# The fallback for crowded experts moved behind the last expert, one-hot matrices right behind the slots, and half of the router's logits amid the output projection

## The chip, the cores and the metric

The kernel runs on one core of a Trainium2 chip. The metric is the device time of one execution in microseconds (us); the time of a kernel is the median of several executions. The profile and the trace come from one further execution that the hardware profiler recorded. Engines are named PE (TensorE, with PEld for its weight loads), DVE (VectorE), ACT (ScalarE), POOL (GpSimd) and SP (SyncE, which here only issues DMAs).

## The reference

256 tokens of 1024 channels go through two layers of four parallel mixers, gates and an output projection, each followed by a feed-forward part (dense in layer 0, a mixture of experts in layer 1), and then through a second block. What the change touches is the end of layer 1's mixers and the experts:

```python
def first_block(x, ...):
    for l in range(2):
        h = _rmsnorm(x, norm_mix[l])
        ...                                   # four mixers, gates: merged
        x = x + merged @ w_out[l]
        h = _rmsnorm(x, norm_ffn[l])
        if l == 0: x = x + _swiglu(h, ffn_w1, ffn_w3, ffn_w2)
        else:      x = x + _moe_ffn(h, router, moe_w1, moe_w3, moe_w2)
    return x

def _moe_ffn(h, router, w1, w3, w2):          # 256 tokens, 8 experts of width 1408
    logits = h @ router
    top_logit, top_idx = lax.top_k(logits, 2)
    gates = softmax(top_logit)
    # each token: sum over its two experts e of gate * (silu(h@w1[e]) * (h@w3[e])) @ w2[e]

def second_block(x, ...):
    h = rms_norm(x, norm_gain)
    proj = h @ w_in                           # "w_in_2" below
    ...
```

Every product is formed to float32's accuracy.

## The kernel before

**Products.** A weight block is loaded by a DMA that SP issues (`raw`), rounded by ACT into a high part `wh` and split by DVE into the rest `wl`. An activation has a high and a low part as well (`mh`, `ml`; `hr` in two halves; `xg`). Each block product is then three PE instructions: high by high, low by high, high by low. All of PE's instructions pass through the helper `mm` or `TE.transpose` (line 123 in the profile); a trace row is told apart by its tiles, the result left of the arrow and the operands right of it. PSUM has banks under two tags, "mm" and "mx", four each. Names in rows of `dense` products: `mh,wh` is w_out, `wh,xg` an expert's first and third matrix, `wh,mu` its second, `nr,wh` and `wh,nr` the second block's w_in_2.

**The end of layer 1's mixers.** `dense` forms `merged @ w_out` in two groups of 512 channels (g = 0, 1); `residual` (L980) adds each to `xT`, which holds the tokens' stream as 8 channel tiles of 128x256. Group 0 gives the tiles 0 to 3, group 1 the tiles 4 to 7.

**The router.** For each channel tile ACT scales it (`hT`, L1393), DVE squares it (`msq`, L1395), two narrow products with the router's table `rt` and with a column constant add to the logits and to the sums of squares, and two transposes put the tile into token rows. All eight tiles go through this behind w_out's last product. ACT copies the sums (`part`), PE folds them (`c_moe,part`), and DVE chooses two experts for each token in a chain of 128x16 operations (L1423 to L1432, ending in the mask `msk`) while POOL forms the norm's factor `mrs` with a power. PE counts with `msk` each token's place in its expert, DVE writes it as `pos`; `cnt` and `cnti` are the largest expert's number of tokens. `hr` is the normalised rows, two halves of width and two of tokens.

**The fallback.** An expert's tokens are gathered into at most 128 places. A path for any number (the body of `tc.If(full > P)`, L1573) is compiled in and stands between the counts and the gates: every engine loads the count `cnti` into a register (L1570) and branches. With these inputs no expert has over 128 tokens and every engine jumps over the body.

**The experts.** `gather` builds for two experts a one-hot matrix `Q` (DVE, L1478) from `pos`, multiplies it with `hr` (PE, `Q,hr`), and casts the result into `xg` (ACT and DVE). `ffn` runs one expert and gives `y` (ACT L1552 and DVE L1553), scaled by the gates `gs`; `scatter` multiplies `y` with the transposed one-hot matrix `pt_` and adds to `xT` (DVE L1568). While expert 7 runs its last blocks, w_in_2's first blocks are loaded already. The second block's norm then squares `xT` (`room`), sums it over the partitions (`ones,room`), takes POOL's power and transposes the factors (`c_id,nrmb`); w_in_2's products with the tiles `nr`, which need no factor, are put around this.

The order on each engine is set by a list scheduler with priorities; `tc.high_priority(offset=...)` lifts instructions, `add_manual_dep` forbids an order, and each engine then works through its row in order.

Of the kernel before, what the change touches and what calls it, by code (L numbers as in the profile page):

```python
# [21 lines left out]
# TensorE takes its instructions in order: (step of the chains, products of the gates put before it)  # L22
# [7 lines left out]
# where each constant lies: name -> (group, first column, columns)  # L30
# [3 lines left out]
def _constants():  # L34
# [12 lines left out]
    for m in (2, 4, 8, 16, 32):  # L47
# [20 lines left out]
           "mfold": np.arange(P)[:, None] % 32 == np.arange(16)[None, :], "col8": np.broadcast_to(np.arange(32) == 8, (P, 32))}  # L68
# [6 lines left out]
    for g, blocks in (("c_id", ident), ("c_mix", mix), ("c_moe", moe), ("c_nsa", nsa)):  # L75
# [25 lines left out]
def build(tc, I, out, dbg=None, upto=99):  # L101
# [15 lines left out]
    # TensorE, with a list of its instructions where one is asked for  # L117
# [18 lines left out]

    last_in = {}
# [69 lines left out]
    def wsplit(raw, k, n, perm=False):  # L207
        """hi / lo tiles [128, k, n] of a loaded [128, k, n] block."""
# [20 lines left out]
        # own slots, the standing ones after the first of them, own slots  # L229
# [41 lines left out]
    def wload_(src, k, n, rows, pinned):  # L271
        """src: DRAM [k*128, n] -> raw tile [128, k, n]."""
# [17 lines left out]
    def wstream(W, c0, cn, K, perm=False, rows=False, raw=None, pre=None):  # L290
        """hi, lo, kc-base, count for the rows of W[:, c0:c0+cn]."""
# [16 lines left out]
    def dense(W, c0, cn, K, act, jobs, perm=False, rows=False, raw=None, pre=None):  # L308
        """jobs: ("T", off, n): out[n cols, 256 tok]; ("R", off, n): out[tok, n] of both token tiles.
        Returns per job an AP: T -> [n, 256], R -> list of two [128, n]."""  # L310
# [3 lines left out]
        for kind, off, n in jobs:  # L314
            if kind == "T":
                if used + T > 512:
                    cur, used = bank("mm"), 0
# [4 lines left out]
            else:  # L322
                aps = []
                for j in range(2 if kind == "R" else 1):
                    if used + n > 512 or n == 512:
                        cur, used = bank("mm"), 0
# [26 lines left out]
    def inv_sqrt(pool, sums, n, mul, add, nm):  # L353
        """PSUM sums [128, n] -> (sums * mul + add) ^ -0.5, or of the larger of both when mul is None."""
# [25 lines left out]
    def head_scale(pool, sq, n, mul, add, nm):  # L380
        """sq [128 = 2 heads x 64, n tokens] -> PSUM [128, n]: the same per head and token."""
# [59 lines left out]
    def ln_rows(mp, y, eps_v, nm):  # L441
        """y: [128, 8, 64] in place: (y - mean) * rstd over the last axis."""
# [32 lines left out]
    def mix_layer(l):  # L475
        with ExitStack() as ls_:
# [4 lines left out]
            branch = {}  # L481
            tmp = lambda shape, nm, tag: mp.tile(shape, F32, name=nm, tag=tag)
# [4 lines left out]
            # ---- projections of the RWKV branch, shifted and mixed  # L487
# [30 lines left out]
            # ---- RWKV: decays and keys, channels on partitions  # L518
# [18 lines left out]
            S.activation(out=ls, in_=ls, func=AF.Exp)            # decay up to the step before  # L537
# [6 lines left out]
            ar = mp.tile([P, 2, 2, 2, P], F32, name="ar")        # [ch, b, token tile, a|r, tok]  # L544
# [18 lines left out]
            # ---- rows of the same  # L563
            br, kr, vr = t2("br", "pt0"), t2("kr", "pt1"), t2("vr", "pt2")       # [tok, tile, channel]
# [13 lines left out]
            def solve(j):  # L578
                """Scores of token tile j and the solve (I - A)^-1 of its two chunks."""
# [15 lines left out]
                # right-hand sides [A~ | Aak V]  # L595
# [30 lines left out]
                # state side, the part without the running state  # L626
                nt = mp.tile([P, 2, 2, 64], F32, name="nt", tag="nt", bufs=2)   # [k', chunk, b, k]
# [21 lines left out]
                # query side  # L649
# [37 lines left out]
            def rows_to_branch(y, i, th, tl):  # L687
                """y [128 tok, (tile, head), 64] -> branch i, transposed, hi/lo."""
# [39 lines left out]
            # ---- projections of the other branches  # L728
# [1050 lines left out]
```

## Time and profile before

| | |
|---|---|
| median of 3 executions | 1457.94 us (1456.82 to 1458.63) |
| profiled execution, span | 1455.6 us |
| PE busy | 1410.7 us, 97% |
| DVE busy | 1092.4 us, 75% |
| ACT busy | 822.3 us, 56% |
| POOL busy | 63.9 us, 4% |
| DMA moved | 294.46 MB, 202 GB/s |

The span is the time from the first to the last instruction of the profiled execution, which is 2.3 us under the median of the three timed ones. A duration in the trace is of that execution. PE rows overlap: a product's row shows 0.28 or 0.39 us, and the next one starts 0.12 or 0.23 us after it, so for PE the starts are read.

### The profile page before, as it was taken

How to read it: one execution, taken by the hardware profiler on the slowest of the kernel's cores; microseconds unless marked ns; L12 is line 12 of the kernel's file. 1: busy time of each engine (PE TensorE's matmuls, PEld its weight loads, DVE VectorE, ACT ScalarE, POOL GpSimd, SP SyncE). 2: the span in 40 equal slices, each digit the busy share in tenths (PEclk: the TensorE clock that was granted, in tenths of full speed). 3: DMA queues.
4: the chain of work that ended last, by engine and by line, in shares of the span. 5: the costliest groups of instructions: out<-in, count | busy, mean ns of one | idle time of the engine just before them, and what ended most of it. 6: DMA issues, size and time to landing. Idle time of an engine off the chain costs nothing. (4 is left out here: it accounts for less than half of the span.)

```text
span 1455.6 us, 25080 instructions
## 1 busy us (share of the span) xinstructions
PE 1410.7 (97%) x10183; PEld 1304.4 (90%) x10183; DVE 1092.4 (75%) x1606; ACT 822.3 (56%) x1169; POOL 63.9 (4%) x82
## 2 busy tenths in 40 slices
PE   5999999999999999999999799999999999999998
PEld 5999999999999899999899688888888887998997
DVE  3759876776655575797676799898898998676665
ACT  4644264564444464433645588788788777465553
POOL 1000010001000100001000000000000001120000
PEclk9999999999999999999999899999999999999999
DMA  7453024576553445421458599899799895843342
GB/s 255 151 176 116 31 92 168 177 290 206 199 186 127 152 132 170 145 84 34 143 182 289 180 359 361 299 358 361 282 371 358 288 340 171 280 142 117 116 117 87
DMA packets 137388, 294.46 MB, mean 202 GB/s; under 512 B 6718, under 2 KB 28614, under 8 KB 137009
## 3 DMA queue, kind: packets, MB, share of 16 engines
q1 hardware_dynamic: 133952, 282.64, 56.3%
q0 software_dynamic: 3232, 10.13, 2.1%
q8 instruction: 81, 1.33, 0.4%
q14 instruction: 43, 0.34, 0.1%
q10 hardware_dynamic: 80, 0.02, 0.0%
HBM read 290.15 MB, written 2.62 MB: 201 GB/s over the span
## 5 line engine op out<-in xcount | busy, mean ns | idle before, releaser
L253 DVE TENSOR_TENSOR wl<-raw,wh 128x1024 fp32r<-128x1024 f32 (+1 forms) x542 | 633.5, 1186 | 221.7 <-ACT wh L252 216.7
L252 ACT CAST wh<-raw 128x1024 fp32r<-128x1024 f32 (+1 forms) x542 | 549.0, 1021 | 384.9 <-PE mm L123 293.2
L123 PE MATMUL mm<-hh,wh 128*128 128x256 f32 x1376 | 395.8, 288 | 4.1 <-ACT hh L1650 3.8
L123 PE MATMUL mm<-hl,wh 128*128 128x256 f32 x1376 | 393.4, 286 | 0.2 <-DVE hl L205 0.2
L123 PE MATMUL mm<-hh,wl 128*128 128x256 f32 x1376 | 392.7, 286 | 0.0
L123 PEld LDWEIGHTS mm<-hh,wh 128*128 128x128 f32 x1376 | 264.3, 192 | 9.7 <-ACT hh L1650 4.0
L123 PEld LDWEIGHTS mm<-hl,wh 128*128 128x128 f32 x1376 | 264.1, 192 | 3.1 <-issue 1.8
L123 PEld LDWEIGHTS mm<-hh,wl 128*128 128x128 f32 x1376 | 264.1, 192 | 2.0 <-issue 1.2
L123 PE MATMUL mm<-wh,xg 128*128 128x512 f32 (+1 forms) x768 | 231.5, 376 | 0.0
L123 PEld LDWEIGHTS mm<-wh,xg 128*128 128x128 f32 x768 | 142.7, 188 | 21.9
L123 PE MATMUL mm<-wl,xg 128*128 128x512 f32 (+1 forms) x384 | 143.9, 375 | 0.0
L123 PE MATMUL mx<-wh,mu 128*128 128x512 f32 x352 | 118.4, 398 | 0.0
L123 PEld LDWEIGHTS mm<-wl,xg 128*128 128x128 f32 x384 | 72.2, 188 | 11.2
L123 PEld LDWEIGHTS mx<-wh,mu 128*128 128x128 f32 x352 | 66.2, 188 | 13.5
L123 PE MATMUL mx<-wl,mu 128*128 128x512 f32 x176 | 69.3, 394 | 0.0
L886 DVE SCALAR_TENSOR_TENSOR cac<-cu,pcd,cac 128x256 f32<-128x256 f32 x120 | 52.2, 476 | 0.0
L123 PE MATMUL mx<-uh,wh 128*128 128x256 f32 x176 | 48.8, 280 | 0.4 <-ACT uh L204 0.4
L123 PE MATMUL mx<-ul,wh 128*128 128x256 f32 x176 | 49.1, 280 | 0.0
L123 PE MATMUL mx<-uh,wl 128*128 128x256 f32 x176 | 49.1, 279 | 0.0
L123 PE MATMUL mm<-nr,wh 128*128 128x256 f32 x192 | 39.3, 302 | 3.4 <-ACT nr L410 1.7
L123 PEld LDWEIGHTS mx<-wl,mu 128*128 128x128 f32 x176 | 33.1, 188 | 5.9
L123 PE MATMUL mm<-mh,wl 128*128 128x256 f32 x128 | 35.9, 281 | 0.0
(681 smaller groups left out, 2183.7 us busy)
## 6 DMA issues: line engine op xcount, KB each, us to landing
raw<-in_moe_w_dram SPq DMA_DIRECT2D x104, 1024.0 KB
raw<-in_w_in_dram SPq DMA_DIRECT2D x44, 1024.0 KB
raw<-in_ffn_w_dram SPq DMA_DIRECT2D x33, 1024.0 KB
raw<-in_w_gate_dram SPq DMA_DIRECT2D x32, 1024.0 KB
raw<-in_moe_w_dram SPq DMA_DIRECT2D x32, 768.0 KB
raw<-in_w_out_dram SPq DMA_DIRECT2D x12, 1024.0 KB
raw<-in_w_branch_dram SPq DMA_DIRECT2D x8, 1024.0 KB
raw<-in_moe_w_dram SPq DMA_DIRECT2D x8, 512.0 KB
```

Source lines behind the costliest of these rows:

```text
L123: i = getattr(nc.tensor, name)(*a, **k)
L252: a = S.copy(out=h, in_=raw)
L253: i = V.tensor_sub(out=o, in0=raw, in1=h)
L886: V.scalar_tensor_tensor(acc[:, b], cu[:, b, 2 + k:2 + k + T], dw[:, 2 * k + b:2 * k + b + 1], acc[:, b], op0=OP.mult, op1=OP.add)
```

## The change

Four things change.

1. The fallback becomes a function `beyond`, called by expert 7's `ffn` between its last product with w2 and its `y`. `y`'s two banks then have the tag "mm", and inside the body `dense` uses "mx". The count's register is loaded under a high priority as expert 7 begins.
2. The first `gather` is started before the gates, at a high priority: `Q` directly behind `pos`. Three of the four low parts of `hr` are forced behind it. The four small operations that give the count move into `gates`.
3. The router's work on the tiles 0 to 3 (`routed(.., 0, ..)`: 4 scalings, 2 squares, 8 narrow products, 8 transposes) is recorded into w_out's group 1 of layer 1, and a manual dependence puts it ahead of that group's last products. The tiles 4 to 7 stay behind.
4. The column constant gets a table of its own (`c_col`). It and the router's table are loaded twice, by POOL's queue, once for each half.

```diff
             for g in range(2):
+                rec[0] = filler = []
                 _, bb = dense(I["w_out"][l], g * 512, 512, KC, (mh, ml), TJ)
+                if g and l == 1:
+                    rec[0] = chain = []
+                    late["routed"] = r_ = {"lg": bank("mm"), "rows": [[bank()] for _ in range(2)]}
+                    half = [mg.tile([P, 512], F32, name="gth", tag="gth", bufs=13) for _ in range(4)]
+                    routed(r_, 0, [x.rearrange("p (a b) -> p a b", b=T) for x in half])
+                    for i in chain:
+                        tc.add_manual_dep(filler[60].ins, i.ins.name, nosync, reason="first half first")
+                rec[0] = None
...
+    def router(pool):
+        late["rt"] = rt = pool.tile([P, KC, 32], F32, name="rt")
+        G.memset(rt, 0.0)
+        nc.gpsimd.dma_start(out=rt[:, :, 0:8], in_=I["router"][0].rearrange("(k p) e -> p k e", p=P))
+        cload("c_col", pool, nc.gpsimd)
+
+    def routed(r_, hf, tiles):
+        lg, rows, rt = r_["lg"], r_["rows"], late["rt"]
+        gain = gains("nf", 1, 2)
+        hT, sq = tiles[:2], tiles[2:]
+        for q in range(2):
+            for c in range(2):
+                k = 4 * hf + 2 * q + c
+                S.activation(out=hT[q][:, c], in_=xT[:, k], func=AF.Copy, scale=gain[:, k:k + 1])
+            V.tensor_tensor(out=sq[q], in0=xT[:, 4 * hf + 2 * q:4 * hf + 2 * q + 2], in1=xT[:, 4 * hf + 2 * q:4 * hf + 2 * q + 2], op=OP.mult)
...
+            lg, rows = late["routed"]["lg"], late["routed"]["rows"]
+            for x in rows:
+                x.append(bank())
+            routed(late["routed"], 1, [hT[:, 2 * q:2 * q + 2] for q in range(2)] + [fp.tile([P, 2, T], F32, name="msq", tag="mth", bufs=3) for _ in range(2)])
...
-                yb = [bank(), bank()]
+                yb = [bank("mm" if other else "mx") for _ in range(2)]
...
+                if other:
+                    other()
                 y = fp.tile([P, 2, D], F32R, name="y", tag="y", bufs=2)
...
-            full = nc.values_load(cnti[0:1, 0:1], min_val=0, max_val=T)
-            held = dict(more), dict(turn)
-            more["few"] = 1
-            with tc.If(full > P):
-                gates()
-                for e in range(8):
...
+            def beyond():
+
+                held = dict(more), dict(turn)
+                more["few"] = 1
+                with tc.If(full > P):
+                    into[0] = "mx"
+                    for e in range(8):
...
             now, nxt, pending = [], [], []
+            with tc.high_priority(offset=400):
+                first = gather(0, 0, now, True)
+                next(first)
+                for r in lows[1:]:
+                    tc.add_manual_dep(r.ins, late["Q"].ins.name, nosync, reason="slots first")
+                for _ in range(7):
+                    next(first)
             gates()
-            run(gather(0, 0, now, True))
+            run(first)
...
+                if e == 7:
+                    with tc.high_priority(offset=300):
+                        full = nc.values_load(cnti[0:1, 0:1], min_val=0, max_val=T)
-                y = ffn(e, now[1][:, i:i + 1], pre, lambda a=ready: scatter(a), steps)
+                y = ffn(e, now[1][:, i:i + 1], pre, lambda a=ready: scatter(a), steps, beyond if e == 7 else None)
```

What this does to the order on the engines, at the places that matter. First PE's row at the end of w_out in the changed kernel (`gth` are the half's tiles there):

```order
L124 MATMUL mm<-mh,wl 128x256
L124 MATMUL mm<-gth,rt 32x256 [waits DMASW4_49,PE_49,Pool_49]
L124 MATMUL mm<-gth,c_col 32x256 [waits DMASW3_49]
L124 MATMUL mm<-gth,rt 32x256
L124 MATMUL mm<-gth,c_col 32x256
...
L124 MATMUL mx<-c_id,gth 128x128 x8
L124 MATMUL mm<-mh,wh 128x256
```

Eight narrow products and eight transposes now stand ahead of the last 18 products of w_out. Behind these 18 come the other eight transposes and eight narrow products, where before all sixteen of each stood.

DVE's row from the choice of the second expert to `Q`, changed kernel:

```order
L255 TENSOR_TENSOR wl<-raw,wh 128x1024 [waits DMAHW2_49,Activation_49]
L1448 TENSOR_TENSOR hot<-c_moe,ix 128x16 [waits DVE_49]
...
L1481 TENSOR_TENSOR g_8917<-mx 128x2
...
L1482 TENSOR_TENSOR g_8917<-g_8917,mrs 128x2 [waits DVE_49,Pool_49]
...
L1453 TENSOR_TENSOR msk<-hot 128x16 [waits DVE_49]
L1471 SCALAR_TENSOR_TENSOR hr_8847<-mx,mrs,hr_8846 128x512 [waits Activation_49]
L1461 SCALAR_TENSOR_TENSOR pos<-mm,msk 128x16 [waits DVE_49,PE_49]
L1477 COPY cnt<-mm 128x16
L1462 TENSOR_SCALAR pos<-pos 128x16 [waits DVE_49]
L1478 TENSOR_TENSOR cnt<-cnt 128x8 [waits DVE_49]
L1501 TENSOR_TENSOR Q<-c_moe,pos 128x512 [waits DVE_49]
```

The same stretch of DVE's row before, from the mask to the branch; the split `wl` stood ahead of the choice there, and the `Q` that is used stands behind the body that is jumped over:

```order
L1432 TENSOR_TENSOR msk<-hot 128x16 [waits DVE_49]
L1452 SCALAR_TENSOR_TENSOR hr_8814<-mx,mrs,hr_8813 128x512 [waits Activation_49]
L1440 SCALAR_TENSOR_TENSOR pos<-mm,msk 128x16 [waits DVE_49,PE_49]
...
L1445 TENSOR_REDUCE cnt<-cnt 128x1 [waits DVE_49]
...
L1447 CAST cnti<-cnt 128x1 [waits DVE_49]
L1570 TENSOR_LOAD cnti [waits DVE_49]
L1573 COMPARE_AND_BRANCH
```

`Q` comes directly behind `pos` in the changed kernel; a split and two small operations for the gates (`g`, the second of which waits for POOL) have come into the choice.

PE's row behind expert 7 in the changed kernel, from the first product of w_in_2 to the transposes of the norm's factors:

```order
L124 MATMUL mm<-nr,wh 128x256 [waits Activation_49]
L124 MATMUL mm<-nr,wh 128x256
L124 MATMUL mm<-nr,wh 128x256 [waits DVE_49]
...
L124 MATMUL mx<-ones,room 128x1 [waits DVE_49,PE_49]
L124 MATMUL mx<-ones,room 128x1 x3
L124 MATMUL mm<-nr,wl 128x256 [waits DVE_49]
L124 MATMUL mm<-nr,wh 128x256 x2
L124 MATMUL mm<-nr,wl 128x256 x2
L124 MATMUL mm<-wh,nr 128x128
L124 MATMUL mm<-wl,nr 128x128
L124 MATMUL mx<-c_id,nrmb 128x128 [waits DVE_49,PE_49]
```

Four products of w_in_2 stand ahead of the sums and seven between the sums and the transposes; before it was 30 and 13. The register's load and the branch stand directly behind expert 7's last product on PE, behind its last `wl` on DVE and its last `wh` on ACT, and ahead of all of `y`, `scatter` and w_in_2's splits; before, one of w_in_2's splits stood ahead of `y`.

## Rows read from the trace of the kernel before

**Rows 1.** Busy time by stretch: us from:to, length, engines' busy, PE's clock, DMA share.

```profile
776.00:798.80 22.80, 22.80 (x197) 22.80 (x196) 14.23 (x18) 9.67 (x14) 0.00 (x0) 1.00 0.94 336
807.00:820.00 13.00, 5.08 (x24) 5.11 (x25) 8.53 (x22) 6.02 (x10) 0.00 (x0) 0.50 0.35 105
823.50:1228.00 404.50, 404.50 (x2009) 346.41 (x2007) 368.71 (x384) 314.62 (x366) 5.65 (x8) 1.00 0.91 326
1228.00:1241.00 13.00, 9.40 (x71) 8.45 (x70) 12.12 (x22) 9.05 (x17) 2.42 (x2) 0.96 0.18 54
1241.00:1247.00 6.00, 6.00 (x31) 6.00 (x30) 5.39 (x11) 2.51 (x5) 3.74 (x10) 0.51 0.99 321
1247.00:1280.00 33.00, 33.00 (x283) 33.00 (x283) 20.66 (x46) 18.87 (x43) 0.00 (x0) 1.00 0.78 275
```

**Rows 2.** PE in order of time, w_out's end to the first expert: start, duration, work.

```profile
798.46 0.28 PE L123 MATMUL mm<-mh,wl 128*128 128x256 f32 x1
...
800.13 0.40 PE L123 MATMUL mm<-hT,rt 128*32 128x256 f32 x1
...
802.14 0.66 PE L123 MATMUL mx<-c_id,hT 128*128 128x128 f32 x4
...
814.92 6.38 PE L123 MATMUL mx<-Q,hr 128*128 128x256 f32 x32 [8.06 <-DVE g L1459]
821.14 0.40 PE L123 MATMUL mm<-wh,xg 128*128 128x512 f32 x1
```

**Rows 3.** DVE in order of time, the same stretch.

```profile
801.47 1.23 DVE L253 TENSOR_TENSOR wl<-raw,wh 128x1024 fp32r<-128x1024 f32 x1
...
805.63 0.17 DVE L1432 TENSOR_TENSOR msk<-hot 128x16 f32<-128x16 f32 x1
...
807.10 0.17 DVE L1441 TENSOR_SCALAR pos<-pos 128x16 f32<-128x16 f32 x1
...
813.35 0.16 DVE L1458 TENSOR_TENSOR g<-mx 128x2 f32<-128x2 f32 x1 [3.90 <-DVEq L1573]
814.08 0.69 DVE L1478 TENSOR_TENSOR Q<-c_moe,pos 128x512 fp32r<-128x512 f32 x1 [0.57 <-PEq L1573]
```

**Rows 4.** ACT in order of time, the same stretch.

```profile
802.27 0.37 ACT L1410 COPY part<-mm 128x256 f32<-128x256 f32 x1 [0.83 <-PE mm L123]
```

**Rows 5.** Register load, branch and join of PE, L1570 and L1573: count, duration ns, start us.

```profile
L1570 PEldq TENSOR_LOAD <-cnti x1: 490/490/490, 809.5 to 809.5; - x1
...
L1573 PEldq COMPARE_BRANCH  x1: 3852/3852/3852, 810.1 to 810.1; - x1
...
L1573 PEldq EVENT_SEMAPHORE  x1: 51/51/51, 814.0 to 814.0; - x1
```

**Rows 6.** DMA queues from 800 to 820 us: packets, MB, share of 16 engines.

```profile
q14 instruction: 6, 0.05, 0.7%
```

**Rows 7.** PE in order of time, behind expert 7.

```profile
1227.72 0.39 PE L123 MATMUL mx<-wh,mu 128*128 128x512 f32 x1
...
1231.18 0.50 PE L123 MATMUL mm<-nr,wh 128*128 128x256 f32 x2 [0.26 <-ACT nr L410]
...
1237.27 1.02 PE L123 MATMUL mx<-ones,room 128*128 128x1 f32 x8 [1.26 <-DVE room L418]
1238.16 0.72 PE L123 MATMUL mm<-nr,wh 128*128 128x256 f32 x4
...
1239.47 0.39 PE L123 MATMUL mm<-wh,nr 128*128 128x128 f32 x2
1240.68 0.66 PE L123 MATMUL mx<-c_id,nrmb 128*128 128x128 f32 x2 [0.82 <-DVE nrmb L374]
```

**Rows 8.** ACT in order of time behind expert 7, the first of its rows.

```profile
1227.45 1.38 ACT L1552 ACTIVATE y<-mx,gs 128x512 fp32r<-128x512 f32 x2 [1.05 <-PE mx L123]
```

**Rows 9.** DVE in order of time, the last split of expert 7.

```profile
1222.80 1.21 DVE L253 TENSOR_TENSOR wl<-raw,wh 128x1024 fp32r<-128x1024 f32 x1
```

**Rows 10.** The kernel's last line, L1775, PE's sequencer: count, duration ns, start us.

```profile
L1775 PEldq DRAIN  x2: 13/2140/4267, 1447.5 to 1455.1; - x2
```

More of the change, by code (lines that the diff above doesn't have):

```diff
@@ L135, in bank @@
         return pp.tile([P, 512], F32, name=tag, tag=tag, bufs=4)
+    into = ["mm"]
     last_in = {}
@@ L481, in mix_layer @@
             branch = {}
+            if l == 1:
+                router(mp)
             tmp = lambda shape, nm, tag: mp.tile(shape, F32, name=nm, tag=tag)
@@ L975, in mix_layer @@
             dump(f"xm{l}", xT)
+    def router(pool):
[12 more added lines that the diff above has]
+            V.tensor_tensor(out=sq[q], in0=xT[:, 4 * hf + 2 * q:4 * hf + 2 * q + 2], in1=xT[:, 4 * hf + 2 * q:4 * hf + 2 * q + 2], op=OP.mult)
+            for c in range(2):
+                k = 4 * hf + 2 * q + c
+                for r, lhs, rhs in ((k % 4, rt[:, k], hT[q][:, c]), ((k + 2) % 4, C("col8"), sq[q][:, c])):
+                    mm(lg, lg[r * 32:r * 32 + 32, :T], lhs, rhs, start=k < 2, stop=k > 5, chain=True)
+        for q in range(2):
+            for c in range(2):
+                for j in range(2):
+                    TE.transpose(rows[j][hf][:, (2 * q + c) * P:(2 * q + c + 1) * P], hT[q][:, c, j * P:(j + 1) * P], ident)
     def residual(aps_banks, c2):
@@ L1378, in moe @@
             xg = fp.tile([P, 2, KC, 2, P], F32R, name="xg")
-            hT = fp.tile([P, KC, T], F32, name="hT", tag="y", bufs=2)
+            hT = fp.tile([P, 4, T], F32, name="hT", tag="y", bufs=2)
             cload("c_moe", fp, nc.gpsimd)
-            rt = fp.tile([P, KC, 32], F32, name="rt")
-            G.memset(rt, 0.0)
-            nc.gpsimd.dma_start(out=rt[:, :, 0:8], in_=I["router"][0].rearrange("(k p) e -> p k e", p=P))
-            msq = [fp.tile([P, 2, T], F32, name="msq", tag="mth", bufs=3) for _ in range(3)]
+            router(fp)
             mu = fp.tile([P, 2, 11, P], F32R, name="mu")
             hr = [ap_.tile([P, 2, D], F32R, name=f"hr{x}", tag=t_, bufs=1) for x, t_ in enumerate(("acth", "actl"))]
-            lg = bank("mm")
-            rows = [[bank() for _ in range(2)] for _ in range(2)]
-            for q in range(4):
-                for c in range(2):
-                    k = 2 * q + c
-                    S.activation(out=hT[:, k], in_=xT[:, k], func=AF.Copy, scale=gain[:, k:k + 1])
-                sq = msq.pop() if msq else fp.tile([P, 2, T], F32, name="msq", tag="mth", bufs=3)
-                i = V.tensor_tensor(out=sq, in0=xT[:, 2 * q:2 * q + 2], in1=xT[:, 2 * q:2 * q + 2], op=OP.mult)
-                if q == 1:
-                    for r in late["residuals"][2:]:
-                        tc.add_manual_dep(r.ins, i.ins.name, nosync, reason="first half first")
-                for c in range(2):
-                    k = 2 * q + c
-                    for r, lhs, rhs in ((k % 4, rt[:, k], hT[:, k]), ((k + 2) % 4, C("col8"), sq[:, c])):
-                        mm(lg, lg[r * 32:r * 32 + 32, :T], lhs, rhs, start=k < 2, stop=k > 5, chain=True)
-                for c in range(2):
-                    k = 2 * q + c
-                    for j in range(2):
-                        TE.transpose(rows[j][k // 4][:, k % 4 * P:(k % 4 + 1) * P], hT[:, k, j * P:(j + 1) * P], ident)
+            lg, rows = late["routed"]["lg"], late["routed"]["rows"]
+            for x in rows:
+                x.append(bank())
+            routed(late["routed"], 1, [hT[:, 2 * q:2 * q + 2] for q in range(2)] + [fp.tile([P, 2, T], F32, name="msq", tag="mth", bufs=3) for _ in range(2)])
             io8 = C("io8").rearrange("p (a b) -> p a b", b=8)
@@ L1496, in gather @@
                         TE.transpose(b_[:, e * T + j * P:e * T + (j + 1) * P], Qf[:, j, e], ident)
-                pt_ = fp.tile([P, 2, T], F32R, name="pt_", tag="pt_", bufs=2)
+                pt_ = fp.tile([P, 2, T], F32R, name="pt_", tag=f"pt_{off}", bufs=1 if off else 2)
                 S.copy(out=pt_.rearrange("p a b -> p (a b)"), in_=b_)
@@ L1507, in gather, with ffn @@
                 yield
-            def ffn(e, gs, pre=(None, None), between=None, steps=None):
+            def ffn(e, gs, pre=(None, None), between=None, steps=None, other=None):
                 w2 = I["moe_w2"][0, e]
```

46 lines of the change are left out of this document (25 added, 21 removed).

## The prediction

> **What bounds the kernel now.** I read the table of stretches first. While w_out's second group runs, and again from expert 0 to the end of expert 7, PE is busy in every microsecond (22.80 of 22.80 and 404.50 of 404.50), while DVE has 62% and 91% and the DMA engines 0.94 and 0.91 [rows 1]. In these stretches an instruction more on PE costs its length; nothing else counts. Between them lie two holes, which PE's row shows in order of time. The first is the router: PE's last w_out product starts at 798.46 and its first product with an expert's weights at 821.14, and the main work in between is the gather, 32 products in 6.38 us from 814.92 [rows 2]. The second lies behind expert 7: from 1228 to 1241 PE has 9.40 us of work in 13.00, and from 1241 to 1280 it is full again [rows 1]. So the time is worked out as the shift of two points: the gather's start, and the moment from which PE is full in the second block.
>
> The clock belongs to both. [...] Both holes remain, so I count the clock the same and put what it could do into the bounds.
>
> **What the branch costs today.** PE loads the count at 809.5 in 0.49 us, its branch takes 3.85 from 810.1, and its join is passed at 814.05 [rows 5]: 4.55 us in all, while PE has nothing else to do. DVE's first work behind the branch starts at 813.35 [rows 3], 3.85 after the loads. An instruction queue moved 6 packets, 0.05 MB, between 800 and 820 [rows 6]. [...]
>
> **The router half amid w_out.** It puts 8 narrow products and 8 transposes ahead of w_out's last 18 products, on an engine without a gap. All 16 narrow products lie between 800.13 and 802.14 today, so half of them cost 1.0 us; four transposes that wait for nothing take 0.66 [rows 2], of which the next work overlaps a part, so eight cost about 1.1 (at most 1.3). Last product of w_out: +2.1. What this takes off behind that product is less clear. Today the sums are ready for ACT 3.81 us after the last product's start (798.46 to 802.27 [rows 2, 4]), by way of residual, scaling, transposes and narrow products. With half of the tiles the last residual and scaling stay, and all of the second half's transposes now stand ahead of its narrow products, where four stood behind them. I take nothing off (bounds: nothing, or the 1.0 us of the narrow products): `part` +2.1, between +1.1 and +2.3.
>
> **The choice.** The split `wl`, which lay at 801.47 beside the narrow products and took 1.23 us, now lies inside the chain of the choice, with two operations of some 0.16 us (as `g` today) [rows 3] and a wait for POOL that no row sizes. I put 1.2 for the split and 0.4 for the rest: the mask is ready 3.5 us behind `part` today (802.27 to 805.80 [rows 3, 4]) and 5.1 then. Bounds of the loss: 0.4, if the split falls into a wait, and 2.0. The mask comes at 798.46 + 2.1 + 3.81 + 5.1 = 809.5.
>
> **Q behind pos, without the branch.** Today Q starts 8.3 us after the mask (805.80 to 814.08), though pos is complete 1.5 after it, at 807.27 [rows 3]. With one small operation between them Q starts 1.6 behind the mask, at 811.1, takes 0.69, and the gather follows 0.15 later as it does today (814.77 to 814.92 [rows 2, 3]): 811.9 instead of 814.92. The low parts of `hr` that were put behind Q have Q's shape and come every 0.7 us or so, and the gather needs 0.8 for four products at the lower clock (6.38 by 32, [rows 2]), so it is not held up; PE works on from there without a gap, as today. **Front: -3.0.** Bounds: with the better ends above (1.0 less in the sums, 1.2 less in the choice) -5.2; with the worse ones and half a microsecond of waiting in the gather -1.9.
>
> **The branch behind expert 7.** Its join must be passed by PE, DVE and ACT before the first `y`, which starts at 1227.45 today [rows 8]. Behind it are queued `y`, the scatter and w_in_2's splits, so the whole way to the second block shifts with it. The question is when each engine meets it. DVE meets it behind expert 7's last split, at 1222.80 + 1.21 = 1224.0 [rows 9], and is through 3.85 later, at 1227.9. PE's load stands behind its last product, which starts at 1227.72 [rows 7]; but the last thing that product's row waits for is the same split, at 1224.0, and PE's sequencer can run ahead of its engine: at the kernel's end its drain lasts 4.27 us from 1447.5 [rows 10], that is, it had handed on all products over 4 us before the last was done. If it does so here, it meets the load at about 1224.4, and 4.55 later, at 1229.0, the join is passed. **Tail: +1.6** (1229.0 less 1227.45). Bounds: +0.4, by DVE alone, and +4.8, if the load or the branch waits until PE's engine has done its work (1227.72 + 4.55 = 1232.3). I take the first reading, since of all rows the drain is nearest to it.
>
> [...]
>
> **The products that filled the second hole.** Today 43 products of w_in_2 run in it, 30 ahead of the sums and 13 behind (the first start at 1231.18, the last row at 1239.47 [rows 7]). In the changed order all of w_in_2's splits stand behind the norm's operations on DVE, and 11 products are left, 4 and 7. The other 32 come after the hole, where PE is full and where a product of this kind costs about 0.116 us (22.80 by 197 in w_out, products of the same size [rows 1]): **+3.7.** Bounds: +1.2, if only one split's length is late and something else sets the pace there; +3.7, if PE has to take all of them without a gap. I take the upper end, since PE is full for 39 us behind the hole [rows 1].
>
> The second loading of the router's table and of the column constant is POOL's, which works 5.65 us in 404.5 [rows 1], and costs nothing as long as it lands ahead of the half amid w_out; if it were late, PE would stop there, and no row prices that.
>
> **Sum.** Profiled span 1455.6 - 3.0 + 1.6 + 3.7 = 1457.9. The median of the timed runs is 2.3 us above the span: 1460.2. What a measurement of this kernel can tell from no change is about 0.2%, 2.9 us: the forecast of +2.3 is no change that can be told, on the slow side.
>
> **Rivals.**
> *PE meets the branch only behind its last product.* That PE's branch record alone is 3.85 us long [rows 5] speaks for some waiting of its own; the drain speaks against it. The tail is then +4.8: -3.0 + 4.8 + 3.7 = +5.5, 1463.4. It decides from 1.3 us of the shift in PE's load on. Chance 0.25.
> *A dear tail besides:* in a longer hole the clock falls before the scatter, and it and the sums run at half of it, some 2 us more, 1465.4. Chance 0.03.
> *The displaced products do not count,* because the DMA engines (0.99 behind 1241 [rows 1]) and not PE set the pace: -3.0 + 1.6 + 1.2 = -0.2, with the better front -2.4: 1455.5 to 1457.7. PE's full row speaks against it. Chance 0.18, of which 0.08 below 1455.0.
> *The front is worth more:* the hole gets short enough for the clock to stay, and the gather's 32 products start every 0.12 us instead of 0.2, another -2.6. With the better front -7.8 + 5.3 = -2.5, 1455.4, and less if the branch is hidden as well. The idle time ahead of the gather is hardly shorter than today's, which speaks against it. Chance 0.16, of which 0.12 below 1455.0.
> The forecast: 0.38, from 1457.5 to 1461.5, of which 0.06 lie above 1460.9.
>
> **Range and chances.** The range takes in the better front at one end and PE's late branch at the other: 1453.5 to 1465. Slower by over 0.2%: 0.25 + 0.03 + 0.06 = 0.34; faster 0.08 + 0.12 = 0.20; the same 0.46.
>
> **What would show it.** Right: no load or branch in the router's stretch and a gather that starts near 812, with the experts behind it without a gap; PE's load 3 to 4 us ahead of its last product's start; `y` 1 to 2 us later behind that product than today; 11 products of w_in_2 ahead of the factors' transposes and a full PE behind them. Wrong: PE's load only behind the last product; a gather that starts after 814; gaps on PE behind the second hole that swallow the displaced products.

## The result and the profile after

The changed kernel takes 1472.66 us (median, 1470.45 to 1474.97), before 1457.99 beside it: a ratio of 1.0103, 95% interval [1.009, 1.0117]. It is slower by 1%, above the whole range. The profiled execution spans 1473.2 us against 1455.6, that is +17.6; it is the longest of four, and 1.5 us of it lie ahead of the places that this document is about: the stage behind layer 0 begins at 509.3 instead of 507.8. That start differs from one profile to the next whatever was changed behind it: it is 506.7 to 509.1 in the kernels below, and 506.9 in e1, which loads the same tables ahead of it as the changed kernel.

Stretches as in [rows 1]: length, busy PE, PEld, DVE, ACT, POOL, clock, DMA share, GB/s.

```profile
778.00:801.80 23.80, 23.80 (x211) 23.08 (x210) 13.75 (x17) 10.07 (x15) 0.00 (x0) 1.00 0.26 91
823.50:1234.50 411.00, 407.63 (x2008) 343.90 (x2006) 366.51 (x389) 303.55 (x363) 5.63 (x8) 1.00 0.91 323
1234.50:1241.00 6.50, 1.34 (x5) 1.26 (x6) 1.35 (x2) 2.08 (x3) 0.00 (x0) 0.82 0.38 131
1241.00:1254.00 13.00, 7.59 (x35) 6.87 (x33) 10.84 (x21) 7.38 (x15) 2.44 (x2) 0.50 0.02 3
```

From 823.50 to the end of expert 7's last product it is 411.0 us, 6.5 more than before, and PE is no longer busy in all of it. PE, router to first expert, and then DVE, the same stretch:

```profile
798.15 0.40 PE L124 MATMUL mm<-gth,rt 128*32 128x256 f32 x1
...
799.15 1.09 PE L124 MATMUL mx<-c_id,gth 128*128 128x128 f32 x8
...
813.81 6.25 PE L124 MATMUL mx<-Q,hr 128*128 128x256 f32 x32 [1.29 <-ACT wh L254]
...
820.25 0.48 PE L124 MATMUL mm<-wh,xg 128*128 128x512 f32 x1
```

```profile
807.86 1.22 DVE L255 TENSOR_TENSOR wl<-raw,wh 128x1024 fp32r<-128x1024 f32 x1
...
810.76 0.18 DVE L1453 TENSOR_TENSOR msk<-hot 128x16 f32<-128x16 f32 x1
...
812.97 0.69 DVE L1501 TENSOR_TENSOR Q<-c_moe,pos 128x512 fp32r<-128x512 f32 x1
```

The gather starts 1.1 us sooner than in [rows 2], 2.6 sooner without the 1.5 that came from ahead: the front does nearly what was forecast. From its start to the start of expert 7's last product it was 412.8 us; now it is 420.3. Waits of PE, then of its weight loads, from 820 to 1240 and to 1235 us (total, times, longest); in before neither `wl` nor `wh` stands in such a list:

```profile
PE mm L124 <- DVE wl L255: 2.4, 4, 0.8
PE mm L124 <- ACT wh L254: 0.7, 2, 0.3
```

```profile
PEld mm L124 <- DVE wl L255: 7.3, 14, 1.2
PEld mm L124 <- ACT wh L254: 1.9, 3, 0.8
```

One such place, expert 2's end, first ACT, then PE:

```profile
966.55 1.05 ACT L254 CAST wh<-raw 128x1024 fp32r<-128x1024 f32 x1 [0.33 <-PE mx L124]
971.43 1.39 ACT L1578 ACTIVATE y<-mx,gs 128x512 fp32r<-128x512 f32 x2 [3.83 <-PE mx L124]
972.72 4.83 ACT L254 CAST wh<-raw 128x1024 fp32r<-128x1024 f32 x5
```

```profile
973.81 0.51 PE L124 MATMUL mm<-wh,xg 128*128 128x512 f32 x1 [0.34 <-ACT wh L254]
975.07 0.50 PE L124 MATMUL mm<-wl,xg 128*128 128x512 f32 x1 [0.75 <-DVE wl L255]
```

ACT stands 3.83 us before a `y` whose products PE has not finished; the splits of the next expert's weights are queued behind it, start all together at 972.72, and PE waits for the first `wh` and then for its `wl`. The order of ACT's row has changed: seven splits where eight stood ahead of this `y`, and other counts around the tanh behind it. ACT's instructions around expert 2's `y`, before and then after:

```
L204 CAST mu<-mx 128x384
L252 CAST wh<-raw 128x1024 x8
L1552 ACTIVATE y<-mx,gs 128x512 x2
L252 CAST wh<-raw 128x1024 x4
L1528 ACTIVATE mth<-mm 128x512
L252 CAST wh<-raw 128x1024 x8
L1528 ACTIVATE mth<-mm 128x512
```

```
L206 CAST mu<-mx 128x384
L254 CAST wh<-raw 128x1024 x7
L1578 ACTIVATE y<-mx,gs 128x512 x2
L254 CAST wh<-raw 128x1024 x5
L1552 ACTIVATE mth<-mm 128x512
L254 CAST wh<-raw 128x1024 x6
L206 CAST mu<-mx 128x512
L254 CAST wh<-raw 128x1024 x2
L1552 ACTIVATE mth<-mm 128x512
```

ACT's waits in the experts, after and then before, show which of its instructions wait. Now they are more often those that take a result of PE (`mth`, `y`, `mu`), with splits queued behind them; before, most of the waiting was done by the splits themselves (`wh`).

```profile
ACT mth L1552 <- PE mm L124: 32.4, 24, 3.1
ACT wh L254 <- PE mm L124: 26.2, 66, 1.6
ACT y L1578 <- PE mx L124: 16.9, 7, 3.8
ACT mu L206 <- PE mx L124: 13.0, 6, 2.9
```

```profile
ACT wh L252 <- PE mm L123: 50.6, 105, 3.7
ACT wh L252 <- PE mx L123: 24.7, 68, 3.1
ACT mth L1528 <- PE mm L123: 7.1, 24, 0.3
ACT y L1552 <- PE mx L123: 2.7, 4, 1.1
```

The tail: PE's branch and its join (the point behind the body, where the engine goes on), ACT's first `y`, then PE in order of time.

```profile
L1600 PEldq COMPARE_BRANCH  x1: 6526/6526/6526, 1232.2 to 1232.2; - x1
L1600 PEldq EVENT_SEMAPHORE  x1: 51/51/51, 1238.8 to 1238.8; - x1
```

```profile
1238.92 1.26 ACT L1578 ACTIVATE y<-mm,gs 128x512 fp32r<-128x512 f32 x2 [10.09 <-PEq L1600]
```

```profile
1234.09 0.40 PE L124 MATMUL mm<-wh,mu 128*128 128x512 f32 x1
1239.66 3.94 PE L124 MATMUL mx<-pt__11803,y 128*128 128x256 f32 x16 [5.18 <-ACT y L1578]
...
1253.66 0.66 PE L124 MATMUL mx<-c_id,nrmb 128*128 128x128 f32 x2 [0.79 <-DVE nrmb L376]
```

PE met its branch ahead of its last product, as forecast, but the branch lasts 6.53 us where it was 3.85 [rows 5], and `y` starts 4.83 us behind that product's start, where it was 0.27 ahead [rows 7, 8]: +5.1. ACT and DVE had passed their joins at 1230.7 and 1232.7, so `y` waits for PE's alone. From `y` to `nrmb` it is 14.7 us (13.2 before), from there to the end 219.5 (214.9): the last block's first piece in the chain that ended last, now and before, holds the displaced products:

```profile
1254.33 48.86 PE mm L124 x397
```

```profile
1241.34 45.48 PE mm L123 x365
```

So: +1.5 from ahead, -2.6 front, +7.5 gather to last product, +5.1 to `y`, +1.5 to `nrmb`, +4.6 to the end: 17.6.

### The profile page after: what moved, and what is told of

It reads as the page before. It is cut to its first block, busy times and chain, and to the rows that moved or that the text cites. A ratio compares the mean times of both kernels' runs of the same rounds, so it can differ in the third digit from the quotient of the medians.

```text
span 1473.2 us, 25068 instructions
## 1 busy us (share of the span) xinstructions
PE 1420.9 (96%) x10183; PEld 1307.6 (89%) x10183; DVE 1090.0 (74%) x1606; ACT 813.9 (55%) x1169; POOL 66.0 (4%) x86
## 4 chain that ended last, share of the span: by engine, by line
PE 87%; DVE 5%; issue 3%; ACT 2%; DMA 1%; POOL 1%; SPq 0%; ACTq 0%; DVEq 0%; POOLq 0%
PE mm L124 61%; PE mx L124 26%; DVE wl L255 2%; DMA raw<-in_w_in_dram 1%; ACT wh L254 1%; DVE cac L890 1%; POOL hss L362 0%; DVE nhf L438 0%; DMA gth<-in_x_dram 0%; POOL tlis L362 0%; POOL nrms L362 0%; DVE xT L1020 0%; DVE xT L1594 0%; POOL lbd L1335 0%; ACT pt L518 0%
## 5 line engine op out<-in xcount | busy, mean ns | idle before, releaser
L254 ACT CAST wh<-raw 128x1024 fp32r<-128x1024 f32 (+1 forms) x542 | 540.3, 1021 | 334.2 <-PE mm L124 268.7
L124 PE MATMUL mx<-wh,mu 128*128 128x512 f32 x308 | 103.7, 398 | 0.0
L124 PEld LDWEIGHTS mx<-wh,mu 128*128 128x128 f32 x308 | 57.7, 188 | 11.5
L124 PE MATMUL mx<-wl,mu 128*128 128x512 f32 x154 | 60.9, 395 | 0.0
L124 PE MATMUL mm<-mh,wh 128*128 128x256 f32 x128 | 36.0, 282 | 0.0
L124 PE MATMUL mm<-ml,wh 128*128 128x256 f32 x128 | 36.0, 281 | 0.0
```

What stands on the lines that cost most here:

```text
L124: i = getattr(nc.tensor, name)(*a, **k)
L254: a = S.copy(out=h, in_=raw)
```

## The experiments

Theories for the experts: *order* (ACT's row, above) and *loads*: the half's tiles lie in memory that the first experts' weights also use, so SyncE's queue is held for 20.8 us from 779, the DMA share amid w_out is 0.26 where it was 0.94 [rows 1], and the weights come later. For the tail: *drain* (PE's branch waits for the products in hand) and *contention* (what the branch fetches, by the author's reading the 6 instruction packets of [rows 6], shares the DMA engines with loads). Before measured 1457.3, 1457.1 and 1457.0 us beside the three sets (e1 to e4, e5 to e8, e9 to e12).

**e1_half_alone**: the changed kernel with the fallback back in the router's stretch and `Q` behind it again; the half and its tables stay.

```diff
+            full = nc.values_load(cnti[0:1, 0:1], min_val=0, max_val=T)
+            beyond()
             now, nxt, pending = [], [], []
-            with tc.high_priority(offset=400):
-                first = gather(0, 0, now, True)
...
-                y = ffn(e, now[1][:, i:i + 1], pre, lambda a=ready: scatter(a), steps, beyond if e == 7 else None)
+                y = ffn(e, now[1][:, i:i + 1], pre, lambda a=ready: scatter(a), steps)
```

> The changed kernel with the fallback back at its old place ahead of the gates, so Q again behind the branch: the half of the router amid w_out and the split tables are all that is left of the change. Order theory (the experts lose 7 us because without a branch ahead of them the scheduler orders them in one block with the mixers, and ACT's row then holds up the splits): the experts' rows are the regular ones again, PE has no gap in them, and only the half's 2 us on PE stay: about 1460. Loads theory (the experts lose 7 us because the first expert loads wait some 20 us for the memory of the half's tiles): the wait is still there, so PE waits for splits in the experts and the time is about 1465 or more.

1463.99 us, ratio 1.0053 [1.0035, 1.0071]. It has the same hold of 20.8 us, and no wait of PE in the experts at all, which speaks against *loads*; but its gather starts 6.5 us later than the changed kernel's and leaves the loads that much more time, so this run alone doesn't settle it. The hold has a price elsewhere: the loads held back run while PE is in its branch (first the stretch 812 to 819 us, columns as in [rows 1], then the branch).

```profile
812.00:819.00 7.00, 0.00 (x0) 0.00 (x0) 0.23 (x2) 0.00 (x0) 0.00 (x0) 0.50 0.92 334
```

```profile
L1600 PEldq COMPARE_BRANCH  x1: 5932/5932/5932, 812.9 to 812.9; - x1
```

PE has nothing in hand there, and the branch is 2.1 us longer than in [rows 5]: the gather starts at 820.29, 5.4 later than before. With that and experts of 407.9 us the time is near 1464 and not the 1460 of *order*.

**e2_no_half**: the changed kernel with all eight tiles of the router behind w_out.

```diff
-                if g and l == 1:
-                    rec[0] = chain = []
...
-                        tc.add_manual_dep(filler[60].ins, i.ins.name, nosync, reason="first half first")
```

> The changed kernel with all eight channel tiles of the router behind w_out again; fallback at the end and Q behind pos stay. Order theory: PE still loses 7 us in the experts, the tail still loses 10, the front gains 2 more: about 1470. Loads theory: the expert loads start as early as before the change, the experts run without a gap: about 1463.

1469.99 us, 1.0081 [1.0065, 1.0098]. The hold is gone, and the waits of weight loads for `wl` stay:

```profile
PEld mm L124 <- DVE wl L255: 6.0, 12, 1.2
```

*Loads* fell as the cause of the stall. From expert 0's first product to expert 7's last it is 411.8 us (413.8 changed, 406.6 before). PE's branch lasts 6.95 us.

**e3_fallback_end_alone**: the kernel before with part 1 of the change alone (`beyond` in expert 7's `ffn`).

> The kernel before with part 1 alone: the fallback at the end of expert 7. PE's branch should again end some 4.3 us after PE's last product, y 5 us late, and w_in_2's products displaced: +10 in the tail. The front gains 3 to 4 by the branch that is gone. Order theory: another 7 in the experts, about 1471. Loads theory: nothing in the experts, about 1464.

1468.3 us, 1.0079 [1.0062, 1.0096]. One part makes three quarters of the loss (11.0 of 14.7 us): waits for `wl` (5.4), a branch of 5.53 us, `y` 4.1 later behind its product, 11 products ahead of `nrmb`. The experts, first product to last, are 409.7 us: +3.1, where *order* had 7 more.

**e4_no_fallback**: the kernel before without the path for experts with over 128 tokens, which it leaves out: no branch.

```diff
-            full = nc.values_load(cnti[0:1, 0:1], min_val=0, max_val=T)
...
-            with tc.If(full > P):
...
```

> The kernel before without any fallback (it leaves out the path for experts with over 128 tokens, which these inputs don't take, and the branch with it). Order theory: the experts' rows change as in the changed kernel although no branch stands anywhere: front -4, experts +7, about 1461. Loads theory or a pure price of the branch: front -4 and nothing else, about 1454.

1458.01 us, 1.0012 [1.0001, 1.0023]. The gather starts 2.8 us sooner, and nothing is won: the waits for `wl` (5.0) are here too, without any branch or hold. The experts are 409.5 us, which takes back what the front gave; *order* had 7 more here as well, and it is 2.9. Common to the changed kernel, e2, e3 and e4 is that the fallback's body does not stand ahead of the experts; there ACT's row in them comes out irregular, and regular in before and e1. ACT's waits with `mth` in the experts tell the two apart, and the loss there goes with them: 7.1 us in before and 7.2 in e1, 22.4 in e4, 24.3 in e3, 28.4 in e2 and 32.4 in the changed kernel, for 2.9, 3.1, 5.2 and 7.3 us more than before in the last four.

**e5_regular_order**: the changed kernel, ACT's row in the experts put into the order of before.

```diff
+            for kind, n in re.findall(r"([wTUXPY])(\d*)", ROWS):
+                for _ in range(int(n or 1)):
+                    i = seen[kind][at[kind]]
+                    at[kind] += 1
+                    if last_ is not None:
+                        tc.add_manual_dep(i.ins, last_.ins.name, nosync, reason="order of before")
+                    last_ = i
```

> The changed kernel, with one thing put back: ScalarE's row in the experts (high parts of the weights, tanh, copies of u, y, gathered x) stands in the order that it has in the kernel before, from the first expert to the last. Branch, counts, Q and router half stay as changed. Order theory: TensorE waits for wl in the experts because ScalarE's splits stand behind a tanh or a copy that is not due yet; with the old order these waits (7.3 + 2.4 + 1.9 + 0.7 us) go, the expert stage is 407 us long or less instead of 413.8, and the time is 1465 to 1467, that is +0.55% beside before. Loads theory (the loads that start after the 20.8 us hold of SyncE's queue are what the splits miss): the waits stay, 1472 to 1473. Clock theory (the early part of the kernel or a lower clock makes the difference): no change in the waits either, 1472.

1465.15 us, 1.006 [1.0046, 1.0074]: 7.5 us less than the changed kernel by the medians, 6.3 by the ratios, with dependences alone. Waits of PE in 820 to 1235 (that for `y` is the tail's), and of weight loads in 820 to 1229 for `wl`, 7.3 in the changed kernel:

```profile
PE mx L125 <- ACT y L1582: 3.9, 1, 3.9
PE mm L125 <- DVE wl L259: 0.7, 1, 0.7
```

```profile
PEld mm L125 <- DVE wl L259: 2.1, 5, 1.2
```

The first product of expert 0 to the last of expert 7 is 407.8 us (413.8 changed, 406.6 before): 6.0 of the 7.3 us are ACT's order, and *order* is shown. The rest of what e5 gains lies behind the experts: its `y` comes 3.55 us behind the last product instead of 4.83, and from `nrmb` to the end it takes 218.5 instead of 219.5.

**e6_no_fallback_regular**: e4 with the same forced order (it leaves out the same path).

> The kernel before without the path for experts with over 128 tokens (left out altogether, no branch on any engine; 1458.0 as the scheduler orders it), with ScalarE's row in the experts in the order of the kernel before. Order theory: the gain of the front (gather at 812.1 instead of 814.9) is no longer eaten in the experts: no waits for wl, expert stage 406.6 instead of 409.5, time 1454 to 1455.5, ratio 0.998. Rival (the experts are bound by the transfers, so that an earlier start only waits longer): 1457.5 to 1458.5, with waits of TensorE for wl of some 5 us as without the forced order.

1452.67 us, 0.9975 [0.9965, 0.9985]; 5.3 less than e4. Of that 3.0 lie in the experts (406.5 us instead of 409.5): the front's gain was real and was eaten there. Another 1.7 lie behind `nrmb`, where a `nr,wl` row of PE lasts 0.28 us from 1.7 us on, and in e4 only from 5.2 us on, 0.41 up to 4.5 (in before and in the changed kernel such a row lasts 0.28 us where the granted clock is 1.00 and 0.41 where it is 0.50); that this is the edit's doing is not shown.

**e7_busy_ahead_of_branch**: the kernel before with six unused products ahead of PE's load and branch.

```diff
+            db = bank("mm")
+            for _ in range(6):
+                mm(db, db[0:8, :], cnt[:, 0], fl(xT[:, 0:2]))
             full = nc.values_load(cnti[0:1, 0:1], min_val=0, max_val=T)
```

> The kernel before, with six products of 8 x 512 in float32 put on TensorE right ahead of its load of the count and the branch in the router's stretch; their sums are used by nothing, and they are added work. [...] Drain theory (TensorE's branch is not taken, or what lies behind it not fetched, until the products ahead of it are done): the branch's record lasts until about 3.9 us behind the end of the last of the six products, and the join comes that much later. Contention theory (in the tail the branch is slow because its fetch shares the DMA engines with loads): the branch takes 3.85 us from its load on, with the products running meanwhile, and the join is passed when they end or before.

One run, 1457.19 us. The added products, then the branch and the join:

```profile
808.78 7.89 PE L123 MATMUL mm<-xT,cnt 128*8 128x512 f32 x12 [1.30 <-DVE cnt L1444]
```

```profile
L1576 PEldq COMPARE_BRANCH  x1: 3372/3372/3372, 810.7 to 810.7; - x1
L1576 PEldq EVENT_SEMAPHORE  x1: 51/51/51, 816.7 to 816.7; - x1
```

PE's sequencer runs ahead of its engine, meets the branch 2 us after these products begin and is through in 3.37 us, while they run: *drain* fell for the branch. Half of it holds for the join, which is passed only at 816.7, when the last product ends (808.78 + 7.89).

**e8_q_ahead_of_branch**: the kernel before, branch in place, counts and first `Q` ahead of it, low parts of `hr` behind both.

```diff
+            with tc.high_priority(offset=400):
+                first = gather(0, 0, now, True)
+                next(first)
+            for r in lows:
+                tc.add_manual_dep(r.ins, late["Q"].ins.name, nosync, reason="slots first")
+            for r in lows:
+                tc.add_manual_dep(r.ins, counted.ins.name, nosync, reason="count first")
             full = nc.values_load(cnti[0:1, 0:1], min_val=0, max_val=T)
```

> The kernel before, with the branch where it was, but the counts and the one-hot matrices Q of the first expert's slots ahead of it on VectorE (right behind pos), and the low parts of hr behind them. The order of the experts stays the one of before but for their first lines. Both theories of the fallback agree on the rest; what is asked is whether part of the front's gain can be had without moving the branch. If Q behind the branch is what holds the gather: the gather starts 1.5 to 2.4 us sooner (812.5 to 813.4), the experts have no waits, time 1455 to 1456, ratio 0.9985. If the hr parts or the branch of TensorE hold it as well: 814.5 to 815.5 and a time of 1457 to 1458.5, no difference.

1455.65 us, 0.9996 [0.9987, 1.0005]: no difference that can be told, though the gather starts at 813.10 and the experts have no waits.

**e9_regular_no_half**: e5 with e2's edit.

> The changed kernel with ScalarE's row in the experts in the order of before (as e5) and, besides, all eight tiles of the router behind w_out again, as in before: no half amid w_out. Asked is what that half is worth by itself. If it costs what it adds on TensorE and gives nothing back: gather near 810.6 instead of 813.6, experts 407 us long, and 1462 to 1463 in place of the 1465.2 of e5. If it gives back behind w_out what it costs: 1465, no difference from e5. If the two faults of the change are only the order and the branch in the tail, this kernel is before with its front 3 to 4 us shorter, its y 3.5 to 5 us later and 3.5 us of displaced products.

1463.39 us, 1.004 [1.0026, 1.0053]: as expected within half a microsecond. The gather starts at 810.96, e5's at 813.62: the half costs the front 2.7 us more than it gives back. In the time it is some 1.8 us, with intervals that overlap.

**e10_quiet_tail**: e5, the loads that SyncE and GpSimd issue behind expert 7 held until its `y`.

```diff
+    def held_load(i):
+        if after_y["left"]:
+            after_y["left"] -= 1
+            tc.add_manual_dep(i.ins, after_y["y"].ins.name, sync, reason="behind y")
+        return i
...
+            after_y.update(y=seen["Y"][-2], left=14)
             scatter(pending)
```

> e5 with the loads that SyncE and GpSimd issue behind the last expert (weights and tables of the layer that follows) made to wait for the last expert's y, so that the DMA engines are idle while TensorE's branch is fetched; the loads come later by that, so the whole time means nothing here. Asked is the length of TensorE's branch record in the tail. Contention theory: 3.4 to 3.9 us as in the router's stretch with idle DMA engines, where it is 6.2 in e5, and y starts some 1.0 to 1.5 us behind the start of the last product (3.6 in e5). Rival (the products that TensorE still has in hand, or the place of the code, make it long): 5.5 to 7 us as in e2, e3, e5 and the changed kernel.

```profile
L1613 PEldq COMPARE_BRANCH  x1: 3626/3626/3626, 1223.6 to 1223.6; - x1
L1613 PEldq EVENT_SEMAPHORE  x1: 51/51/51, 1227.3 to 1227.3; - x1
```

```profile
1226.60 0.40 PE L133 MATMUL mm<-wh,mu 128*128 128x512 f32 x1
1228.17 2.50 PE L133 MATMUL mx<-pt__11803,y 128*128 128x256 f32 x16 [1.17 <-ACT y L1590]
```

The same three microseconds in e5 and then in e10, columns as in [rows 1]:

```profile
1225.00:1228.00 3.00, 3.00 (x15) 2.40 (x14) 0.00 (x0) 0.00 (x0) 2.10 (x4) 1.00 1.08 336
1225.00:1228.00 3.00, 2.00 (x9) 1.28 (x7) 0.00 (x0) 0.57 (x1) 0.00 (x0) 1.00 0.03 8
```

The branch takes 3.63 us with the DMA engines at 0.03 of their time, 6.25 in e5, where the share is 1.08; both meet it 3 us ahead of the last product. `y` starts 0.83 behind that product (3.55 in e5). The branch is longer with loads beside it, and *contention* is shown as far as that; which step of the branch the loads hold up is not. PE's hole ahead of the scatter is 1.2 us here, and the granted clock is 1.00 from 1222 to 1232: the scatter takes 2.50 us instead of the changed kernel's 3.94. One run, 1461.56 us.

**e11_splits_ahead_of_y**: e5 with w_in_2's first two splits ahead of the last `y` on ACT and DVE.

```diff
+            if late.get("ahead"):
+                late["ahead"] -= 1
+                tc.add_manual_dep(late["yA"].ins, a.ins.name, nosync, reason="split ahead of y")
+                tc.add_manual_dep(late["yV"].ins, i.ins.name, nosync, reason="split ahead of y")
```

> e5 with the first two splits of w_in_2, high parts on ScalarE and low parts on VectorE, put ahead of the last expert's y, in the time in which both engines wait for TensorE's branch. Some 40 products of w_in_2 can then run ahead of the factors' transposes, as in before, instead of 11. Displaced products theory: the stretch from the factors' transposes (nrmb) to the end takes 214 to 215 us instead of 218.5, and the time is 1461 to 1462 instead of 1465.2. Rival (that stretch is paced by the transfers or by something else behind it): 1464.5 to 1465.5, and the stretch to the end grows as the transposes come sooner or later.

1461.15 us, 1.0024 [1.0014, 1.0035], 4.0 less than e5. 46 products run ahead of `nrmb`; the chain's piece behind it is

```profile
1249.50 43.61 PE mm L125 x362
```

against 49.28 us for 397 in e5, and from `nrmb` to the end it is 212.7 us instead of 218.5. That is not the 35 products alone, for which the prediction's 0.116 us each give 4.1: PE's rows have the lengths that go with a clock of 1.00 (0.27 or 0.28 us for `wl,nr` and `nr,wl`) from 2.8 us behind `nrmb` on, and in e5 a `nr,wl` row is still 0.41 us 5.6 us behind it. `y` comes 2.0 later behind the last product, since ACT, whose first instruction behind its join again waits for PE's, does the two splits ahead of it; from `y` to `nrmb` it takes 1.0 longer.

**e12_count_then_q**: e8 with the whole count ahead of `Q`.

```diff
+            tc.add_manual_dep(late["Q"].ins, counted.ins.name, nosync, reason="count first")
```

> The kernel before with the branch where it was, the count ahead of the first expert's Q and both ahead of the branch on VectorE (e8 had Q between the two steps of the count). The count is ready some 0.6 us sooner, TensorE's branch of 3.4 to 3.9 us with it, and the gather starts at 812.4 to 812.8 (813.1 in e8, 814.92 in before): 1454.5 to 1455.5. Rival: something besides TensorE's join holds the gather, or what is gained is given back behind it: 1456 to 1457.5, no difference from before.

1454.1 us, 0.9983 [0.9974, 0.9992]: the only kernel that does all the work and beats before, by 2.9 us. DVE and then PE:

```profile
808.15 0.15 DVE L1447 CAST cnti<-cnt 128x1 int32<-128x1 f32 x1
808.22 0.68 DVE L1480 TENSOR_TENSOR Q<-c_moe,pos 128x512 fp32r<-128x512 f32 x1
```

```profile
812.94 5.46 PE L123 MATMUL mx<-Q,hr 128*128 128x256 f32 x24 [5.51 <-DVEq L1585]
818.20 0.63 PE L123 MATMUL mm<-wh,xg 128*128 128x512 f32 x1
```

`Q` is built while PE loads the count (808.3 to 808.8), ahead of the branch (from 808.9) instead of behind it. The gather starts 13.8 us behind w_out's last product, where it was 16.5 [rows 2], and the experts are full (402.00 of 402.00 us from 823.5). Not all of the 2.9 is the front's: in this profile the experts, first product to last, are 1.2 us longer than in before, and the way from `nrmb` to the end is 1.8 shorter, with PE's rows at the lengths of a clock of 1.00 from 3.1 us behind `nrmb` on, where in before the granted clock is 0.50 for 6 us (1240.60 to 1246.60). The two medians of e8 and e12 are 1.5 us apart with intervals that overlap.

## Why the prediction was wrong

**Experts "without a gap": the step that failed most.** The sum has no term for the experts: it took it that PE works on from the gather "without a gap, as today", since PE was full there [rows 1]. But the fallback's body no longer stands ahead of them, and with that ACT's row in them came out in another order: +7.3 us between expert 0's first and expert 7's last product. e5 takes back 6.0 of it by the order alone, and e4 and e6 show 3.0 of the same kind without a branch. The rows of order ahead of the prediction show the places where code had moved, and not the experts. None of the rivals had a term there either, and the highest of them, 1465.4, stays 7 us below the measured time. Why the scheduler orders it so without the body ahead was not tried.

**Tail +1.6: the size failed, the reading held.** PE's sequencer does run ahead: it meets the branch 1.9 us (e5 2.9) ahead of the last product's start, and 2.7 were forecast (1227.72 less 1224.4 and the 0.6 from load to branch [rows 5]); its load at 1231.5 is 2.6 ahead, where the prediction looked for 3 to 4. The step that fell is "4.55 later, at 1229.0": it took the branch's 3.85 us [rows 5] from a place where the DMA share is 0.06 (810.10 to 813.95) to one where it is 0.74 (1232.20 to 1238.80). It was 6.53, and `y` +5.1. With quiet DMA engines (e10) the shift is 0.83 + 0.27 = +1.1, within the term. The rival "PE meets the branch only behind its last product" had the right price, +4.8, by a mechanism that e7 and e10 refute. The prediction had the packets of an instruction queue beside the branch [rows 6], and no step of its tail asks what else the DMA engines carry at the new place.

**"Both holes remain, so I count the clock the same": off by about 1.5.** PE stands 5.2 us ahead of the scatter, and from 1241 to 1254 the granted clock is 0.50, where from 1228 to 1241 it was 0.96 [rows 1]. The scatter's 16 products take 3.94 us, 2.7 before (1228.20 to 1230.92), and the sums 1.83 instead of 1.02 [rows 7]. From `y` to `nrmb` +1.5. In e10, with the scatter at full clock and the sums at 0.50 (1.84 us), half of that is left: 14.0 us from `y` to `nrmb`. That is the "dear tail" rival, which had 2 us and a chance of 0.03.

**Displaced products +3.7: the reading right, the size too small.** Eleven products stand ahead of `nrmb`, as forecast. The chain's piece grew by 3.4, the whole way from `nrmb` by 4.6, above the term's upper bound. The profile before is, besides, at the long end of its kind: in the eight kernels with 43 or more products ahead of `nrmb` the way to the end takes 212.2 to 214.9 us (mean 213.4), in the six with 11 it takes 217.9 to 219.6 (mean 218.8). So the term is nearer 5; 3.7 of it are the products at 0.116 us, and what the rest is stays open. e11 puts 35 products back and takes 5.8 off that way, some of it the clock's.

**Front -3.0: right, -2.6.** The half put w_out's last product off by 2.2 (2.1 forecast: 3.65 later than in [rows 2], less 1.49 by which w_out's first one was late), took nothing off behind (`part` 3.95 behind the last product, 3.81 before), the choice cost 1.35 (1.6 forecast: `part` to the mask's end 4.88 instead of 3.53), `Q` came 2.0 behind the mask (1.6 forecast; a low part of `hr` slipped ahead of `pos`). Not in the sum was that the half holds SyncE's queue 20.8 us; in the experts that shows no price (e5 has the hold, e9 hasn't, and their experts are 407.8 and 407.6 us), at a branch it does (e1).

On the medians: 1460.2 forecast + 7.3 experts + 3.5 tail + 1.5 clock + 0.9 end + 0.4 front = 1473.8, against 1472.66.

## What to carry to other kernels

When a change moves a large block, compare the order on every engine in the stages that it does not touch, ACT's and DVE's among them: on an engine that takes its work in order, an instruction placed one too early waits for its data with everything behind it, as ACT's `y` did for 3.83 us. A jump over a large body has no fixed price (here 3.4 to 7.0 us): read it where the DMA engines are as busy as they will be at the new place, and rather put independent work beside the branch where it is (e12) than the branch beside other work.

## What the runs showed of the hardware

PE's branch over the large body took 3.37 us (e7, e8), 3.63 (e10) and 3.85 (before) with the DMA share beside it at 0.00 to 0.08, whether PE had products in hand (e7, e10) or not; in e12, at the place of before, it took 3.61. With loads running it took 5.93 (e1, share 0.92 from 812 to 819), 6.25 (e5, share 1.08 from 1225 to 1228 and 0.83 from 1228 to 1230) and 6.53 (the changed kernel, share 0.74 over the branch); in the other kernels that have it in the tail with the loads there 5.53 (e3), 5.89 (e9), 6.35 (e11) and 6.95 (e2). In the changed kernel the instruction queues moved 8 packets, 0.08 MB, between 1226 and 1240. ACT's and DVE's records of the same branch are 50 and 72 ns; their joins follow 2.9 and 3.1 us behind it in before and 6.1 and 6.3 in e1. In e7, one run, PE's join is passed at 816.7, when the products handed on ahead of the branch are done.
